# Scores on 64 rows that alternate between the lower and the upper rows of the array

## The chip, the cores and the metric

The kernel runs on one core of a Trainium2 chip. The metric is the time of one execution on the device in microseconds (us). Before the change three runs gave 2135.87, 2143.86 and 2138.03 us, median 2138.03.

The engines are TensorE (PE: matmuls; its weight loads are shown as PEld), VectorE (DVE), ScalarE (ACT), GpSimd (POOL) and SyncE (SP, which issues the loads). They run side by side, each works through its own instructions in order, and a semaphore holds an instruction until what it needs is there.

## The reference

Two transformer blocks of two layers each for 256 tokens of 1024 values, all float32. The change lies in the second block. Each of its layers runs three mixers on one normalised input and joins them:

```python
u = jnp.einsum('btd,de->bte', rmsnorm_2(x, norm1_g[l]), w_in[l])
y_m = mlstm_mixer(...)      # 4 heads of 64: S = (q k^T) * exp(D - m), h = S v / max(|sum S|, exp(-m))
y_a = diff_attention(...)   # 4 heads, each with two halves c of 64:
                            #   p_c = softmax(where(q_pos >= k_pos, q_c k_c^T, -1e30)); o = (p_0 - lam * p_1) v
y_h = hgrn2_mixer(...)      # 4 heads of 64: A[t,s] = sum_k q[t,k] k[s,k] exp(B[t,k] - B[s,k]); o = A v
x = x + concat([y_m, y_a, y_h]) @ w_out[l]
x = x + relu(rmsnorm_2(x, norm2_g[l]) @ w_up[l])**2 @ w_down[l]
```

Each of the scores is a product over 64 values: 64 of the array's 128 rows.

## The kernel before, in words

A weight comes in pieces (`piece`): one DMA into `wraw` (L215), then ScalarE rounds it to `whi` (L226) and VectorE subtracts for the rest, `wlo` (L227). Every large product is three passes of such parts: `gemm_tok` (L247) with tokens on the rows of the result, `gemm_a` (L281) transposed. Their results lie in PSUM banks of the tag "acc"; all small products use the four banks of the tag "sm" (`bank`). A fifth "sm" product must wait until the oldest one's reader is done.

`_second` runs one layer's mixers. A string, `SECOND[l]`, names the order in which the program is written: products (hqf, aq, mvo, ...) and, between them, steps of three generators. `s` is a step of `hgrn_scores`, `a` one of `attention`, `m` one of `mlstm_out`. This is only the written order: the kernel is built with a scheduler (`TileContext(schedule_with_timeline_sim=True)`) that sets the order of the instructions of every engine from its own estimate of times, with the written order as its start. So a change in how a step is written can move its neighbours too.

The operands of two heads, or of the two halves of an attention head, lie above each other: partitions 0 to 63 and 64 to 127. A product over 64 values therefore uses the lower or the upper 64 rows of the array.

- `hgrn_scores`: first `E` and four products per layer (L1540: two on the lower rows into one bank, two on the upper into another), copied by ScalarE (L1541). Then eight levels. A level takes the difference of decay sums (`E`, L1551, L1552), its exponential (ACT, L1553), a product (L1555), and then for the lower rows four matmuls into a bank (L1566) and VectorE's masked copy into `hS` (L1572), and the same again for the upper rows. The last level uses q and k without `E` (`hT`), with 128 columns instead of 64 (copy L1574).
- `mlstm_out`: for each head two matmuls (L1630 256 columns, L1631 128) into one bank and VectorE's product with the weights `wm` (L1632). After two heads come the six products with v (L1638 to L1640).
- `attention`: for each head and each half g: scores of the first 128 queries (L1681), the mask added by a bf16 product of an identity and a matrix of -1e30 (L1682), scores of the other 128 (L1683, 256 columns), the mask (L1684); then VectorE's maximum (L1685, L1686) and bias (L1688) and ScalarE's exponentials (L1690). After both halves the tail of the head before: three transposes of `aa` (L1704), ScalarE's copy `at` (L1706), three products with v (L1708 to L1710), copies (L1712); then the reciprocal of the sums (L1695) and `aa` (L1699). The last head's tail is a step of its own.

After the mixers come `xm`, split from the three outputs (transposes L297), and the product with `w_out`.

Of the kernel before, what the change touches and what calls it, by code (L numbers as in the profile page):

```python
# [10 lines left out]
F32 = mybir.dt.float32  # L11
# [9 lines left out]
D = 1024  # L21
# [3 lines left out]
# ---------------------------------------------------------------- weight pieces  # L25
# A piece is rows [k0, k0 + nk) (in tiles of 128) and columns [c0, c0 + w) of a
# weight, laid out [128, nk, w].
# [45 lines left out]
# ---------------------------------------------------------------- constants of the shapes  # L73
def _consts():
# [19 lines left out]
    for b in (64, 32, 16, 8, 4, 2, 1):  # L94
        j = i[i // b % 2 == 1]   # the queries of this level
        lv.append((i[:, None] // (2 * b) == j[None, :] // (2 * b)) & (i[:, None] // b % 2 == 0))
# [28 lines left out]
# The order of the first block's mixer: products (gt: gates; c, q, v: the delta rule's k, q, v; R, V: retention's q and k,  # L125
# v; g: its output gate; m: merge gates; b: retention's branch; z: the delta rule's output gate), steps of retention (r)
# and of the delta rule (u, k0, L, lv, o, y).
# [4 lines left out]
# The order of the second block's mixer, in its two layers: products (hqf: hgrn2's q, f; hig: its i, g; mvo, mqk: mLSTM's;  # L132
# aq, ak, av: attention's), and steps of hgrn2's scores (s), of attention (a) and of mLSTM (m).
# [4 lines left out]
# Rows of gains, in the order of their use.  # L138
# [4 lines left out]
class Split:  # L143
    """A float32 operand as the sum of two float32r parts."""
# [5 lines left out]
class Kernel:  # L150
# [45 lines left out]
    # ---- weights  # L196
    def piece(self, w, k0, c0, pool=None):
        """Loads a piece of a weight and splits it; with a pool: loads it there, for a later call."""
# [39 lines left out]
    def gemm_tok(self, x, wt, o, tok, k0=0, start=True, stop=True, passes=(0, 1, 2)):  # L238
        """o = x[tok tile] @ w, three passes of float32r parts."""
# [10 lines left out]
    def gemm_b(self, x, w, c0, cb, width=256, n=2, tt=False):  # L250
        """cb(t, x[tok tile t] @ w[:, c0:c0 + n * width]); tt: the first tokens first"""
# [17 lines left out]
    def gemm_a(self, x, wt, ps, first=False):  # L269
        """ps[:, n * 256:+256] = (x @ w[:, n * 128:+128]).T for two n; first: the parts that are ready last come last"""  # L270
# [13 lines left out]
    # ---- activations  # L284
# [5 lines left out]
    def tsplit(self, src, x, t, nk=8, k0=0, scale=None):  # L290
        """x[:, k0:k0+nk, tok tile t] = split(src.T)"""
# [24 lines left out]
    def row(self, name, queue=None):  # L316
        """A vector on all partitions; the next one's load starts."""
# [5 lines left out]
    def rsqrt(self, x, n, scale=1.0, eps=EPS, name="rq"):  # L323
        """(x * scale + eps) ** -0.5 for a narrow x, by Newton's iteration."""
# [17 lines left out]
    def mean_sq(self, x, sq=None):  # L342
        """The mean of x^2 for x [128, D]; sq is overwritten."""
# [25 lines left out]
    def norm_later(self, g, rs, xs=None, sq=(None, None), mid=None):  # L369
        """h * g, transposed (and in xs as it is); rs gets the factors of the tokens that are still to come."""  # L370
# [16 lines left out]
    def along_tokens(self, rs, dg=None):  # L387
        """The factors of the tokens along the columns, on all partitions."""
# [12 lines left out]
    def norm_twice(self, g0, g1, rs):  # L401
        """h = norm(h) * g0; h * g1, transposed, and the factors of its norm."""
# [19 lines left out]
    # ---- first block: mixer  # L422
# [11 lines left out]
    def _mixer(self, l):  # L434
# [5 lines left out]
        if l:   # the factors of the norm come with the products  # L440
# [30 lines left out]
        # ---- the gates of the delta rule, and the first columns of the merge gates  # L471
        gx, beta = one([128, 2, 8], "gx"), one([128, 16], "beta")
        m1 = t8("m1", "xc")   # the merge gates: tanh(x / 2)
# [10 lines left out]
        # ---- the delta rule's k, q, v: convolution, silu, norms  # L484
# [3 lines left out]
        def conv(nm, i):  # L488
# [33 lines left out]
            if nm == "q":  # L522
# [10 lines left out]
                if i == 3:  # L533
                    # of |q|^2, with q's dk ** -0.5
                    G["rq"] = self.rsqrt(qss, 16, scale=128.0, eps=128 * EPS, name="rqq")

        # ---- retention: q, k with rotary, transposed; v; heads
# [58 lines left out]
        # ---- the output gate of retention  # L596
# [13 lines left out]
        # ---- the merge gates, times the branch of retention  # L610
# [22 lines left out]
        # ---- the delta rule's output gate, and its branch  # L633
# [1216 lines left out]
```

## Time and profile before

| | |
|---|---|
| runs, us | 2135.87, 2143.86, 2138.03; median 2138.03 |
| profiled execution, span | 2134.6 us (first to last instruction; no other time of this execution is recorded) |
| instructions | 37091 |
| busy | PE 97%, PEld 90%, DVE 72%, ACT 56%, POOL 2% |
| granted TensorE clock, mean | 0.973 |

The span is read as the time in which the core worked; the runs lie 1.3 to 9.2 us above it. A granted clock of 1.00 is 2.4 GHz and 0.50 is 1.2 GHz. The two mixers of the second block lie at about 1488 to 1560 us (layer 0) and 1840 to 1915 us (layer 1). In a row of the timeline "x2" is the number of hardware instructions: a float32 matmul makes two, a bf16 or float32r matmul one. "64\*128 64x256" is an operand of 64 rows and 128 columns in the array, and 64 rows by 256 columns that stream through it.

### The profile page before, as it was taken

What the parts mean: (1) busy time and instruction counts of PE and PEld (TensorE: products, weight loads), DVE (VectorE), ACT (ScalarE), POOL (GpSimd) and SP (SyncE); (2) the same over time, 40 slices, a digit from 0 to 9 for tenths busy, and PEclk for the clock granted to TensorE, in tenths of its full rate; (3) what the DMA queues carried; (4) which work ended last, traced back from release to release, by engine and by line L of the source; (5) the groups of instructions that cost most, each with busy time, mean ns of one, the idle gap of its engine ahead of it and who ended that gap; (6) DMA issues with size and microseconds to landing.
All of it is one profiled execution on the core that took longest, in us unless ns stands there. A gap on an engine that the chain in (4) does not pass through costs nothing. (4 is left out here: it accounts for less than half of the span.)

```text
span 2134.6 us, 37091 instructions
## 1 busy us (share of the span) xinstructions
PE 2064.5 (97%) x14774; PEld 1928.6 (90%) x14774; DVE 1529.1 (72%) x2848; ACT 1202.5 (56%) x1796; POOL 39.5 (2%) x95
## 2 busy tenths in 40 slices
PE   7999999999999999989999999899899999999999
PEld 7999999999899999988898988789789999888988
DVE  5889576555767996778888888877765448776444
ACT  6554344444564544467787777666535556554554
POOL 0000000000000000000000000020000003000000
PEclk9999899999999999999999999999889999889999
DMA  6454434555544453648999899654225555223553
GB/s 227 161 187 160 127 139 176 195 185 190 188 165 160 175 161 112 218 160 305 332 321 316 322 319 336 233 173 153 80 89 183 193 180 195 101 80 138 181 195 138
DMA packets 82661, 408.14 MB, mean 191 GB/s; under 512 B 25376, under 2 KB 25536, under 8 KB 46768
## 3 DMA queue, kind: packets, MB, share of 16 engines
q1 hardware_dynamic: 61200, 392.19, 51.6%
q0 software_dynamic: 3392, 9.11, 1.4%
q10 hardware_dynamic: 17888, 4.39, 1.0%
q8 instruction: 118, 1.93, 0.4%
q14 instruction: 63, 0.52, 0.1%
HBM read 403.56 MB, written 2.10 MB: 190 GB/s over the span
## 5 line engine op out<-in xcount | busy, mean ns | idle before, releaser
L227 DVE TENSOR_TENSOR wlo<-wraw,whi 128x1024 fp32r<-128x1024 f32 (+3 forms) x644 | 734.4, 1155 | 373.3 <-ACT whi L226 346.5
L226 ACT ACTIVATE whi<-wraw 128x1024 fp32r<-128x1024 f32 (+3 forms) x644 | 633.5, 1005 | 563.7 <-PE acc L247 294.2
L247 PE MATMUL acc<-whi,uhi 128*128 128x256 f32 (+4 forms) x2240 | 609.4, 301 | 9.2 <-ACT uhi L301 4.0
L247 PE MATMUL acc<-wlo,uhi 128*128 128x256 f32 (+4 forms) x2240 | 598.8, 299 | 5.3 <-DVE wlo L227 5.1
L247 PE MATMUL acc<-whi,ulo 128*128 128x256 f32 (+4 forms) x2240 | 602.9, 298 | 0.8 <-DVE ulo L305 0.6
L247 PEld LDWEIGHTS acc<-whi,uhi 128*128 128x128 f32 x2240 | 403.5, 193 | 19.5 <-ACT whi L226 6.6
L247 PEld LDWEIGHTS acc<-wlo,uhi 128*128 128x128 f32 x2240 | 398.2, 191 | 15.2 <-DVE wlo L227 11.4
L247 PEld LDWEIGHTS acc<-whi,ulo 128*128 128x128 f32 x2240 | 400.2, 191 | 5.7 <-DVE ulo L305 1.8
L281 PE MATMUL sm<-uhi,whi 128*128 128x256 f32 x864 | 237.7, 285 | 0.0
L281 PE MATMUL sm<-ulo,whi 128*128 128x256 f32 x864 | 235.9, 282 | 0.0
L281 PE MATMUL sm<-uhi,wlo 128*128 128x256 f32 x864 | 235.1, 281 | 0.0
L227 DVE TENSOR_TENSOR wlo<-xraw,whi 128x704 fp32r<-128x704 f32 (+1 forms) x176 | 165.9, 977 | 38.3 <-ACT whi L226 34.1
L226 ACT ACTIVATE whi<-xraw 128x704 fp32r<-128x704 f32 (+1 forms) x176 | 144.6, 861 | 48.9 <-PE acc L247 14.7
L281 PEld LDWEIGHTS sm<-uhi,whi 128*128 128x128 f32 x864 | 163.8, 195 | 1.6
L281 PEld LDWEIGHTS sm<-ulo,whi 128*128 128x128 f32 x864 | 160.6, 190 | 1.7
L281 PEld LDWEIGHTS sm<-uhi,wlo 128*128 128x128 f32 x864 | 160.4, 189 | 0.0
L247 PE MATMUL acc<-whi,hlo 128*128 128x512 f32 x344 | 135.8, 395 | 0.0
L247 PE MATMUL acc<-wlo,hhi 128*128 128x512 f32 x344 | 135.6, 394 | 0.0
L247 PE MATMUL acc<-whi,hhi 128*128 128x512 f32 x344 | 130.1, 394 | 0.0
L281 PE MATMUL acc<-uhi,whi 128*128 128x256 f32 x448 | 127.3, 284 | 0.0
L281 PE MATMUL acc<-ulo,whi 128*128 128x256 f32 x448 | 126.9, 283 | 0.0
L281 PE MATMUL acc<-uhi,wlo 128*128 128x256 f32 x448 | 126.8, 283 | 0.0
(608 smaller groups left out, 2758.4 us busy)
## 6 DMA issues: line engine op xcount, KB each, us to landing
wraw<-in_w_in SPq DMA_DIRECT2D x80, 1024.0 KB, 4.8
wraw<-in_w_up SPq DMA_DIRECT2D x32, 1024.0 KB, 4.7
wraw<-in_w_down SPq DMA_DIRECT2D x32, 1024.0 KB, 4.7
xraw<-in_exp_w_down SPq DMA_DIRECT2D x24, 1024.0 KB, 7.2
xraw<-in_exp_w_gate SPq DMA_DIRECT2D x32, 704.0 KB, 5.6
xraw<-in_exp_w_up SPq DMA_DIRECT2D x32, 704.0 KB, 5.6
wraw<-in_exp_w_gate SPq DMA_DIRECT2D x32, 704.0 KB, 5.6
wraw<-in_exp_w_up SPq DMA_DIRECT2D x32, 704.0 KB, 5.9
```

Source lines behind the costliest of these rows:

```text
L226: nc.scalar.activation(hi[:, :mm], raw[:, s], AF.Copy)
L227: nc.vector.tensor_tensor(lo[:, :mm], raw[:, s], hi[:, :mm], OP.subtract)
L247: nc.tensor.matmul(o, a[:, k0 + j, ts], b[j], start=start and i == 0 and j == 0, stop=stop and i == 2 and j == n - 1)
L281: self.nc.tensor.matmul(ps[:, n * 256:(n + 1) * 256], a[j][:, n * 128:(n + 1) * 128], b[:, j, :], start=(n, j, i) == one, stop=(n, j, i) = ...
```

## The change

The loops over the row halves go inside: a matmul on the lower rows is followed by the same one on the upper rows. For that both "sm" banks of a pair are taken ahead of the first matmul, and what reads them comes after both. In the attention the four mask products of a head stand together behind its four score products. The rest of the diff removes comments and docstrings, which shifts the line numbers (L1566 is L1567 after it, L1630 and L1631 are L1636, L1632 is L1638, L1681 and L1683 are L1687, L1682 and L1684 are L1690, L1704 is L1712).

```diff
 hgrn_scores
+        ps = [self.bank("sm") for _ in range(2)]
+        for ct in range(2):
+            for pa in range(2):
+                rs = slice(pa * 64, pa * 64 + 64)
+                nc.tensor.matmul(ps[pa][:, ct * 128:(ct + 1) * 128], E3[rs, ct, 0:128], E3[rs, ct, 128:256], start=True, stop=True)
         for pa in range(2):
-            ps = self.bank("sm")
-            rs = slice(pa * 64, pa * 64 + 64)
-            for ct in range(2):
-                nc.tensor.matmul(ps[:, ct * 128:(ct + 1) * 128], E3[rs, ct, 0:128], E3[rs, ct, 128:256], start=True, stop=True)
-            nc.scalar.activation(S2[:, pa], ps[:, 0:256].rearrange("p (c i) -> p c i", c=2), AF.Copy)
+            nc.scalar.activation(S2[:, pa], ps[pa][:, 0:256].rearrange("p (c i) -> p c i", c=2), AF.Copy)
...
+            two = [self.bank("sm") for _ in range(2)]
+            for j in range(4):
+                js = slice(j * 128, (j + 1) * 128)
+                for pa in range(2):
+                    rs = slice(pa * 64, pa * 64 + 64)
+                    nc.tensor.matmul(two[pa][:, j * n:(j + 1) * n], A[rs, js], half(E[rs, js]) if b else fq[rs, js],
+                                     start=True, stop=True)
             for pa in range(2):
-                ps = self.bank("sm")
-                rs = slice(pa * 64, pa * 64 + 64)
-                for j in range(4):
-                    js = slice(j * 128, (j + 1) * 128)
-                    nc.tensor.matmul(ps[:, j * n:(j + 1) * n], A[rs, js], half(E[rs, js]) if b else fq[rs, js], start=True,
-                                     stop=True)
+                ps = two[pa]
                 if b:
 mlstm_out
-            rs_ = slice(pa * 64, pa * 64 + 64)
-            ps = self.bank("sm")
-            nc.tensor.matmul(ps[:, 0:256], mT["k"][rs_, ct, 0:128], mT["q"][rs_, ct, :], start=True, stop=True)
-            nc.tensor.matmul(ps[:, 256:384], mT["k"][rs_, ct, 128:256], mT["q"][rs_, ct, 128:256], start=True, stop=True)
-            nc.vector.scalar_tensor_tensor(wm[:, h, :], ps[:, 0:384], 64.0 ** -0.5, wm[:, h, :], op0=OP.mult, op1=OP.mult)
+            if not pa:
+                two = [self.bank("sm") for _ in range(2)]
+                for o, x, y in ((slice(0, 256), slice(0, 128), slice(0, 256)), (slice(256, 384), slice(128, 256), slice(128, 256))):
+                    for i in range(2):
+                        rs_ = slice(i * 64, i * 64 + 64)
+                        nc.tensor.matmul(two[i][:, o], mT["k"][rs_, ct, x], mT["q"][rs_, ct, y], start=True, stop=True)
+                for i in range(2):
+                    nc.vector.scalar_tensor_tensor(wm[:, h + i, :], two[i][:, 0:384], 64.0 ** -0.5, wm[:, h + i, :], op0=OP.mult, op1=OP.mult)
 attention
+            two = [self.bank("sm") for _ in range(2)]
+            for s, x, y in ((slice(0, 128), slice(0, 128), slice(0, 128)), (slice(128, 384), slice(128, 256), slice(0, 256))):
+                for g in range(2):
+                    gs = slice(g * 64, (g + 1) * 64)
+                    nc.tensor.matmul(two[g][:, s], aT["q"][gs, h, x], aT["k"][gs, h, y], start=s.start == 0, stop=False)
             for g in range(2):
-                gs = slice(g * 64, (g + 1) * 64)
-                ps = self.bank("sm")
-                q, k = aT["q"][gs, h, :], aT["k"][gs, h, :]
-                nc.tensor.matmul(ps[:, 0:128], q[:, 0:128], k[:, 0:128], start=True, stop=False)
-                nc.tensor.matmul(ps[:, 0:128], idb, negb, start=False, stop=True)
-                nc.tensor.matmul(ps[:, 128:384], q[:, 128:256], k, start=True, stop=False)
-                nc.tensor.matmul(ps[:, 256:384], idb, negb, start=False, stop=True)
+                for s in (slice(0, 128), slice(256, 384)):
+                    nc.tensor.matmul(two[g][:, s], idb, negb, start=False, stop=s.start > 0)
+            for g in range(2):
+                ps = two[g]
                 nc.vector.tensor_reduce(mx[:, g, :], ps[:, 0:384].rearrange("p (b i) -> p b i", b=3), axis=AX.X, op=OP.max)
```

The number of instructions of every engine is the same. Up to the second block's first mixer every engine's order is the same too; from there on PE, VectorE and ScalarE differ, POOL and SP do not. Three places show how. In all of them a number behind a name is that of a buffer: two "sm" numbers are two banks, and a bank belongs to one row half.

PE in layer 1, the scores of the first attention head (`aq`, `ak`; `negb`, `idb` are the mask's product), before:

```order
L1681 MATMUL sm_24991<-ak_24438,aq_24641 128x128
L1682 LDWEIGHTS idb_90
L1682 MATMUL sm_24991<-negb_91,idb_90 128x128
L1683 MATMUL sm_24991<-ak_24438,aq_24641 128x256
L1684 LDWEIGHTS idb_90
L1684 MATMUL sm_24991<-negb_91,idb_90 128x128
L1681 MATMUL sm_25001<-ak_24438,aq_24641 128x128
L1682 LDWEIGHTS idb_90
L1682 MATMUL sm_25001<-negb_91,idb_90 128x128
L1683 MATMUL sm_25001<-ak_24438,aq_24641 128x256
L1684 LDWEIGHTS idb_90
L1684 MATMUL sm_25001<-negb_91,idb_90 128x128
```

and after:

```order
L1687 MATMUL sm_24991<-ak_24438,aq_24641 128x128
L1687 MATMUL sm_24992<-ak_24438,aq_24641 128x128
L1687 MATMUL sm_24991<-ak_24438,aq_24641 128x256
L1687 MATMUL sm_24992<-ak_24438,aq_24641 128x256
L1690 LDWEIGHTS idb_90
L1690 MATMUL sm_24991<-negb_91,idb_90 128x128
L1690 LDWEIGHTS idb_90
L1690 MATMUL sm_24991<-negb_91,idb_90 128x128
```

Behind these rows the same two masks follow for the other bank. Heads 0 and 2 of layer 1 stand so; head 1 of layer 1 and head 1 of layer 0 stand with the two products of the lower rows ahead of the two of the upper, and the four masks behind them.

PE in layer 0, levels 0 (its second block) and 1 of `hgrn_scores` (`E`) and the first half of attention head 0, before:

```order
L1566 MATMUL sm_21293<-E_21282 128x64 x4
L1566 MATMUL sm_21304<-E_21299 128x64 x4
L1566 MATMUL sm_21310<-E_21299 128x64 x4
L1681 MATMUL sm_21323<-ak_20959,aq_20565 128x128
L1682 LDWEIGHTS idb_90
L1682 MATMUL sm_21323<-negb_91,idb_90 128x128
L1683 MATMUL sm_21323<-ak_20959,aq_20565 128x256
L1684 LDWEIGHTS idb_90
L1684 MATMUL sm_21323<-negb_91,idb_90 128x128
L281 MATMUL acc_21631<-uhi_20207,whi_21623 128x256
```

and after, from the last two products of the level on:

```order
L1567 MATMUL sm_21304<-E_21299 128x64
L1567 MATMUL sm_21305<-E_21299 128x64
L1687 MATMUL sm_21323<-ak_20959,aq_20565 128x128
L1687 MATMUL sm_21323<-ak_20959,aq_20565 128x256
L1690 LDWEIGHTS idb_90
L1690 MATMUL sm_21323<-negb_91,idb_90 128x128
L1690 LDWEIGHTS idb_90
L1690 MATMUL sm_21323<-negb_91,idb_90 128x128
L281 MATMUL acc_21631<-uhi_20207,whi_21623 128x256
```

The level alternates between its two banks. The scheduler has put the other half of this head (bank sm_21324) twelve large products later, so here one half has both its products and then both its masks. Heads 2 and 3 of layer 0 and head 3 of layer 1 are split in the same way, with other products or the first half's masks between.

VectorE at the end of layer 0's mixer (`amx`, `anb`: maxima and biases of the last attention head; `wm`: mLSTM's scores; `hg`, `E`: hgrn2; `aw`: the reciprocals), before:

```order
L1685 TENSOR_REDUCE amx_21502<-sm_21515 128x3
L1446 TENSOR_SCALAR hx_21859<-acc_21732,r01_20329 128x256
L1686 TENSOR_TENSOR amx_21502<-amx_21502 128x1
L1448 TENSOR_TENSOR hg_20405<-hx_21826,sg_21829 128x256
L1632 SCALAR_TENSOR_TENSOR wm_20930<-sm_21699,wm_20930 128x384
L1686 TENSOR_TENSOR amx_21502<-amx_21502 128x1
L1688 SCALAR_TENSOR_TENSOR anb_21503<-amx_21502,ars_20402 128x2
```

and after:

```order
L1693 TENSOR_REDUCE amx_21502<-sm_21506 128x3
L1552 TENSOR_TENSOR E_21871<-hT_20397 128x256
L1553 TENSOR_TENSOR E_21871<-hT_20397 128x256
L1694 TENSOR_TENSOR amx_21502<-amx_21502 128x1
L1448 TENSOR_TENSOR hg_20405<-hx_21863,sg_21866 128x256
L1694 TENSOR_TENSOR amx_21502<-amx_21502 128x1
L1696 SCALAR_TENSOR_TENSOR anb_21503<-amx_21502,ars_20402 128x2 x2
L1556 TENSOR_TENSOR E_21871<-E_21871,hT_20397 128x512
L1638 SCALAR_TENSOR_TENSOR wm_20930<-sm_21699,wm_20930 128x384
L1638 SCALAR_TENSOR_TENSOR wm_20930<-sm_21700,wm_20930 128x384
L1703 RECIPROCAL aw_21504<-osum_21317 128x4
```

`wm` stood ahead of the maximum and the bias of the second half; it now stands, for both heads, behind them and ahead of the reciprocal.

## Rows read from the trace of the kernel before

**Rows 1.** The page: its span and the busy time of the engines.

```profile
span 2134.6 us, 37091 instructions
...
PE 2064.5 (97%) x14774; PEld 1928.6 (90%) x14774; DVE 1529.1 (72%) x2848; ACT 1202.5 (56%) x1796; POOL 39.5 (2%) x95
```

**Rows 2.** Windows: us, busy PE, PEld, DVE, ACT, POOL, clock, DMA share, GB/s.

```profile
1488.90:1529.50 40.60, 40.60 (x324) 34.96 (x324) 32.73 (x80) 23.84 (x57) 0.00 (x0) 1.00 0.23 81
1529.50:1556.60 27.10, 21.19 (x91) 17.87 (x90) 16.38 (x65) 8.21 (x24) 0.00 (x0) 0.50 0.11 40
1847.10:1898.00 50.90, 50.90 (x395) 45.21 (x393) 39.82 (x109) 29.44 (x70) 0.00 (x0) 0.97 0.29 98
1898.00:1913.00 15.00, 12.64 (x74) 11.68 (x73) 11.89 (x48) 4.60 (x12) 0.00 (x0) 0.62 0.25 91
```

**Rows 3.** Waits of PE in 1529:1557: us in total, times, longest us.

```profile
PE sm L1704 <- DVE aa L1699: 4.7, 1, 4.7
PE sm L1708 <- ACT at L1706: 1.2, 2, 0.6
```

**Rows 4.** Waits of PE in 1898:1913.

```profile
PE sm L1638 <- DVE wm L1632: 2.4, 2, 1.3
```

**Rows 5.** Timeline, PE, layer 0: start us, us, line, operation, operands [idle before].

```profile
1496.33 0.49 PE L1681 MATMUL sm<-ak,aq 64*128 64x128 f32 x2
1496.74 0.23 PE L1682 MATMUL sm<-negb,idb 128*128 128x128 bf16 x1
1496.90 0.70 PE L1683 MATMUL sm<-ak,aq 64*128 64x256 f32 x2
1497.53 0.23 PE L1684 MATMUL sm<-negb,idb 128*128 128x128 bf16 x1
1497.57 0.36 PE L281 MATMUL acc<-uhi,whi 128*128 128x256 f32 x1
...
1498.45 1.60 PE L1566 MATMUL sm<-E 64*128 64x64 f32 x16
1499.98 0.38 PE L281 MATMUL acc<-uhi,whi 128*128 128x256 f32 x1
```

**Rows 6.** Timeline, PE, layer 0: one block of a level by itself.

```profile
1522.91 1.10 PE L1566 MATMUL sm<-E 64*128 64x64 f32 x8
1523.95 0.38 PE L247 MATMUL acc<-whi,uhi 128*128 128x256 f32 x1
```

**Rows 7.** Timeline, PE, layer 1: attention head 0 starts, the level behind it.

```profile
1854.58 0.49 PE L1681 MATMUL sm<-ak,aq 64*128 64x128 f32 x2
...
1857.31 1.60 PE L1566 MATMUL sm<-E 64*128 64x64 f32 x16
```

**Rows 8.** Timeline, PE, layer 1: the scores of two mLSTM heads.

```profile
1898.07 0.71 PE L1630 MATMUL sm<-mq,mk 64*128 64x256 f32 x4
1898.61 0.39 PE L1631 MATMUL sm<-mq,mk 64*128 64x128 f32 x4
```

**Rows 9.** Timeline, PE, the end of layer 0's mixer.

```profile
1529.47 0.76 PE L1704 MATMUL sm<-c_base,aa 128*128 128x128 f32 x3
...
1532.39 1.22 PE L1630 MATMUL sm<-mq,mk 64*128 64x256 f32 x2
...
1538.78 0.99 PE L1704 MATMUL sm<-c_base,aa 128*128 128x128 f32 x3 [4.75 <-DVE aa L1699]
...
1553.61 3.09 PE L1566 MATMUL sm<-hT 64*128 64x128 f32 x16
```

**Rows 10.** Timeline, VectorE, the end of layer 0's mixer.

```profile
1531.26 0.54 DVE L1685 TENSOR_REDUCE amx<-sm 128x3 f32<-128x384 f32 x1
...
1534.07 0.56 DVE L1632 SCALAR_TENSOR_TENSOR wm<-sm,wm 128x384 f32<-128x384 f32 x1 [1.48 <-PE sm L1631]
...
1537.74 0.18 DVE L1695 RECIPROCAL aw<-osum 128x4 f32<-128x4 f32 x1 [0.17 <-ACT pp L1690]
```

**Rows 11.** Timeline, ScalarE, the last head's first exponential.

```profile
1534.81 0.46 ACT L1690 ACTIVATE pp<-sm,anb,ars 128x128 f32<-128x128 f32 x1 [1.02 <-DVE anb L1688]
```

## Prediction

> **What bounds the kernel now.** I read the page's first lines first: TensorE (PE) is busy 2064.5 of 2134.6 us, 97%, VectorE 72%, ScalarE 56% [rows 1]. The change touches only the second block's two mixers, so the stretches in which its lines stand are what counts, and I took the windows there next. In 1488.9–1529.5 (layer 0) and 1847.1–1898.0 (layer 1) PE is busy in all of the time, VectorE in 32.73 of 40.6 and 39.82 of 50.9 us, and the granted clock is 1.00 and 0.97, the 2.4 GHz level [rows 2]: there a microsecond less of PE is a microsecond less of span, as long as nothing else comes late. In 1529.5–1556.6, the end of layer 0's mixer, PE is busy 21.19 of 27.1 us at a granted clock of 0.50, the 1.2 GHz level; in 1898.0–1913.0, the end of layer 1's, 12.64 of 15.0 at 0.62 [rows 2]. The waits of PE in these two name what it waits for: once, 4.7 us, for VectorE's `aa` (the last head's attention weights) [rows 3], and twice, 2.4 us in all, for VectorE's `wm` (mLSTM's weighted scores) [rows 4]. So there are two kinds of term: PE's own time in the full stretches, and a chain over VectorE and ScalarE at the end of layer 0.
>
> **What the array does with 64 rows before the change.** An attention half takes, by the starts of PE's rows, 0.41 us from its first 64-row matmul to the mask, 0.16 to the second 64-row matmul, 0.63 to the second mask and 0.04 to the next full-row product: 1.24 in all [rows 5]. The second 64-row matmul has 128 columns more and takes 0.63 − 0.41 = 0.22 more, so 128 columns cost 0.22 (float32 goes in two passes: x2), and 0.41 − 0.22 = 0.19 is the turn from 64 to 128 rows. Two halves that stand together before the change, with a level behind them, take 1857.31 − 1854.58 = 2.73 [rows 7]. For a level of hgrn2 (8 matmuls, 16 passes), lower block and upper block one after the other take 1499.98 − 1498.45 = 1.53 [rows 5]; one block by itself takes 1523.95 − 1522.91 = 1.04 [rows 6]. Two would be 2.08 in a row, so half of the overlap that the change wants is there already. Two mLSTM heads of 384 columns each, on opposite rows, take 0.93 from the first start to the last end (1898.07 to 1898.61 + 0.39) [rows 8]; by the 0.22 above one of them is 3 × 0.22 = 0.66 of streaming, so they run nearly side by side, although they are written one head after the other.
> The Trainium skill (TensorE: Matmul & The Clock Gate, Part 3: Packing small matmuls — row/col tiling) says that matmuls start and end strictly in program order and that only the loading of weights is pulled ahead. The 0.93 disagrees: upper-row passes start beside lower-row ones that stand ahead of them. By the rule the two attention heads that end up together but not alternating would cost about 0.5 each more, and the sum below would be 1.0 smaller; I go by the trace.
>
> **The change part by part.** No instruction is added or removed; matmuls and weight loads are the same, and the order on PE, VectorE and ScalarE differs only from layer 0's second mixer on.
> 1. *Attention heads whose halves stand together after it* (layer 0 head 1; layer 1 heads 0, 1, 2). Price of a head: 0.93 for two lots of 384 columns [rows 8] and four masks that follow each other, 0.06 each for 128 bf16 columns (bounds: 0.04 by the mask-to-product step, 0.16 by the mask-to-scores step [rows 5]): 1.17. Before: 2 × 1.24 = 2.48 where other products lie between the halves, 2.73 where they are adjacent. Two of each: 2 × 1.31 + 2 × 1.56 = 5.7. With the masks at 0.16: 4.1.
> 2. *Heads that the order still splits* (layer 0 heads 0, 2, 3; layer 1 head 3): 8 halves, in which the two 64-row matmuls now follow each other. Saved is one turn, 0.19, and 0.16 − 0.06 before the second: 0.29 at most, 0.10 at least; I take 0.25, since the 0.19 is the nearer row. 8 × 0.25 = 2.0 (0.8 to 2.3).
> 3. *Levels* (numbered 0 to 7 in their order). Four, level 2 of layer 0 and levels 2, 3, 6 of layer 1, go from block after block to alternating: each from 1.53 to at least 1.04, taken as 1.08, so 4 × 0.45 = 1.8. In layer 0, levels 3 and 4, which overlap each other already, give 0.3, and level 5, whose blocks were apart, 0.5 (bounds 0 and 1.04). Level 0 of layer 0 and levels 1 and 4 of layer 1 stay split by the order, layer 1's level 4 with one block more standing alone; against it stand level 1 of layer 0 and level 5 of layer 1, which now alternate: nothing, with −0.4 to +0.5 around it. The level on hT in layer 0 runs at half clock, 3.09 [rows 9]: eight passes of 128 columns at half clock are 8 × 0.22 = 1.76 of streaming for each row half, side by side and with the offset of two 2.2, so 0.8 with the row's own tail left out. Sum 3.4 (1.8 to 4.5).
> 4. *The end of layer 0.* Before: the transposes of head 2 start on PE at 1529.47, those of the last head at 1538.78, 9.31 later, of which 4.75 idle [rows 9]. In that time VectorE does the last reduce at 1531.26, then reaches `wm`, which waits 1.48 for PE's scores until 1534.07 [rows 10]; behind it in the queue stand the maxima and biases that the exponentials need, so these start only at 1534.81 [rows 11]; 2.93 later, at 1537.74, VectorE takes the reciprocal of their sums, and 1.04 after that PE goes on. After: both `wm` stand behind the biases. The exponentials can start at 1532.1, 0.3 after the reduce's end (1531.26 + 0.54), an estimate: of the two subtractions for E that now stand ahead of the biases nothing is added, since the weight split that stood between the two reduces has moved away. Then the reciprocal is due at 1535.03 and PE at 1536.07. What is late next is `wm` itself: two of 0.56, ahead of the reciprocal and behind both heads' scores, which end at about 1532.39 + 2 × 0.93 (half clock) = 1534.25, so 1535.4 and PE at 1536.4. Of 1538.78 − 1536.4 = 2.4 I take all (bounds: 1.48, the wait alone, and 3.0). The second head's scores, which before followed the last head (one head: 1538.78 − 4.75 − 1532.39 = 1.64 [rows 9]), now lie in PE's idle time: 1.6 more. The other pair joins: 0.2. Sum 4.2.
> 5. *The end of layer 1.* The last head's value products lose the full-row products that lay between them and the transposes, and wait for ScalarE's copy as they do in layer 0, 0.6 each time [rows 3]: −0.6. `wm` comes earlier; of a wait of 2.4 [rows 4] I take 0.95 back. Net +0.35 (−0.6 to +1.8).
> 6. *New waits.* Both banks of a pair are now taken before the first is read, and a bank's reader, the copy to hS or the reduce, comes up to one block later. Behind a PE that waits there stand all the products of its queue. The cover is the lead that VectorE has at 81% and 78% of the two stretches [rows 2]; gone once in each mixer, this costs about one block's half: −1.0 (0 to −4).
> Sum: 5.7 + 2.0 + 3.4 + 4.2 + 0.35 − 1.0 = 14.65, taken as 14.5. The profiled execution spans 2134.6; its own time beyond that isn't recorded. The median of the runs, 2138.03, lies 3.4 above it, and I keep that: 2134.6 − 14.5 + 3.4 = 2123.5. All bounds low: 4.1 + 0.8 + 1.8 + 1.5 + 1.6 − 0.6 − 4 = 5.2; all high: 5.7 + 2.3 + 4.5 + 4.8 + 1.8 = 19.1.
>
> **The rivals.**
> *A. PE only comes sooner to what others have not done.* VectorE at 81% and the weight halves it splits for every product lie in the same stretches [rows 2]; where they have no lead, PE's shorter scores turn into waits, and of parts 1 to 3 (11.1) little is left. Against it: PE waits for nothing in either full stretch. Left are parts 4 and 5 and some of the rest, about 5: 2133.
> *B. It doesn't do what it says.* The order splits four of eight heads and some levels, and the array already lets opposite rows overlap [rows 8]. If joined heads go no faster either, parts 1 and 3 vanish and the waits of 6 remain: −2, 2136. Against it: the turns of 0.19 are real rows [rows 5].
> *C. Slower: the clock falls sooner.* The granted clock is 1.00 up to 1529.5 with PE busy throughout and 0.50 behind it, where PE waits [rows 2]. Row halves side by side, and waits between them, leave PE less occupied in the same stretch. Work of x us at full clock that then lies at half takes x more: it decides from x = 14.5 on, that is if the fall comes at 1515 rather than 1529.5. With both mixers' last 13 us at half: 2123.5 + 26 = 2150. Against it: the products between the scores are untouched, and 0.97 stood through layer 1's scores.
> *D. More.* All bounds at their good end, and with the shorter idle time the clock comes back sooner within the 27.1 us at 0.50: −21, 2117.
>
> **How the numbers follow.** Forecast 0.56, A 0.24, B 0.06, C 0.05, D 0.09. A run of this kernel tells 0.5%, 10.7 us, from no change: faster means under 2127.3, slower over 2148.7. The forecast's own range is 2118 to 2129, with 0.04 of its chance above 2127.3; so faster is 0.52 + 0.09 + 0.03 (of A) = 0.64, slower 0.05 (C), same 0.31. The range reaches from D to A: 2113 to 2135.
>
> **What would show it.** Right: the attention scores of layer 1's heads 0 to 2 and layer 0's head 1 take about 1.2 us from the first 64-row matmul to the next full-row product; a level takes about 1.1; PE's wait for `aa` in layer 0 falls from 4.7 to about 2, with the exponentials' start no longer behind `wm`; and PE's busy time falls by about 11. Wrong: new PE waits for hS, `amx` or weight halves in the full stretches (A); joined heads at 2.4 (B); a granted clock of 0.50 before the last head's scores (C).

## The result, and the profile after

The changed kernel took 2113.06 us (median of five runs, 2111.22 to 2118.89) against 2138.03: ratio 0.989, 95% interval 0.9871 to 0.9909. So it is faster, as forecast, by 25 us where 14.5 were forecast. Over 60 runs of the kernel before, taken beside the experiments below, and 11 of the changed one, the mean spans are 2138.2 and 2112.5 us, and the mean granted clocks 0.9740 and 0.9809.

The page's first lines after (busy us, share of the span, instructions), beside [rows 1]:

```profile
span 2117.1 us, 37095 instructions
...
PE 2048.4 (97%) x14774; PEld 1916.2 (91%) x14774; DVE 1528.7 (72%) x2848; ACT 1203.8 (57%) x1796; POOL 39.9 (2%) x95
```

PE is busy 16.1 us less, where the prediction said about 11; the other engines do what they did. This profiled execution is the slowest of the five runs.

The windows after, with the columns of [rows 2]: layer 0's mixer up to head 2's transposes, its end, and layer 1's mixer up to the last head's transposes, and its end (the third window starts with the mixer, the one in [rows 2] 7.3 us into it):

```profile
1485.50:1521.07 35.57, 35.50 (x323) 31.57 (x322) 33.35 (x82) 25.14 (x61) 0.00 (x0) 1.00 0.30 106
1521.07:1543.72 22.65, 19.34 (x98) 17.04 (x99) 15.52 (x64) 7.47 (x22) 0.00 (x0) 0.58 0.12 44
1826.10:1878.30 52.20, 52.20 (x467) 48.80 (x467) 46.00 (x128) 35.09 (x78) 0.00 (x0) 1.00 0.32 111
1878.30:1893.60 15.30, 11.24 (x91) 10.26 (x90) 13.77 (x53) 7.06 (x17) 0.00 (x0) 0.88 0.28 105
```

From the first S2 product to the first product of hgrn2's output, layer 0's mixer takes 58.2 us (1485.51 to 1543.72) instead of 69.5 (1488.89 to 1558.40), layer 1's 67.5 instead of 74.9: 18.7 us less in the mixers, where the spans differ by 17.5. In layer 1 the two stretches do not hold the same work: 184 full-row products of L247 stand in it after, 166 before, because the first S2 product now stands ahead of 18 of them. At 0.12 us each that is 2.1 us, so for the same work the mixers are about 20.8 us shorter. The full stretches are still full, with VectorE now at 94% and 88%, and PE waits for no semaphore in them. At the end of layer 0 the clock is 0.58 instead of 0.50, at the end of layer 1 0.88 instead of 0.62 [rows 2].

Part of that last gain has only moved. The first 10 us behind layer 1's mixer, before and then after:

```profile
1914.71:1924.71 10.00, 10.00 (x56) 8.69 (x56) 7.54 (x35) 3.90 (x6) 0.00 (x0) 0.97 0.01 2
```

```profile
1893.63:1903.63 10.00, 10.00 (x37) 8.94 (x37) 5.58 (x31) 1.89 (x4) 0.00 (x0) 0.50 0.01 2
```

The clock now falls later (at 1890 us, 11.7 after the last head's transposes start, where before it fell 6 after them) and stays low behind the mixer. From there to the end of the program the changed kernel takes 223.5 us instead of 219.9.

PE's timeline after in layer 1, attention head 0 and the level behind it (start us, us, line, operation, operands), beside [rows 7]:

```profile
1841.40 0.93 PE L1687 MATMUL sm<-ak,aq 64*128 64x128 f32 x8
1842.25 0.40 PE L1690 MATMUL sm<-negb,idb 128*128 128x128 bf16 x4
1842.58 1.11 PE L1567 MATMUL sm<-E 64*128 64x64 f32 x16
1843.62 0.39 PE L281 MATMUL acc<-uhi,whi 128*128 128x256 f32 x1
```

The head takes 1842.58 − 1841.40 = 1.18 instead of 2.73, the level 1.04 instead of 1.53 [rows 5]. In layer 0, the second half of head 0, split from the first, and level 2:

```profile
1492.42 0.92 PE L1687 MATMUL sm<-ak,aq 64*128 64x128 f32 x4
1493.27 0.28 PE L1690 MATMUL sm<-negb,idb 128*128 128x128 bf16 x2
1493.36 0.36 PE L281 MATMUL acc<-uhi,whi 128*128 128x256 f32 x1
...
1494.36 1.11 PE L1567 MATMUL sm<-E 64*128 64x64 f32 x16
1495.40 0.38 PE L281 MATMUL acc<-ulo,whi 128*128 128x256 f32 x1
```

A half takes 0.94 instead of 1.24 [rows 5]. PE's waits at the end of layer 0 and then of layer 1 (us in total, times, longest), beside [rows 3, 4]:

```profile
PE sm L1712 <- DVE aa L1707: 1.6, 1, 1.6
PE sm L1716 <- DVE amx L1693: 0.7, 1, 0.7
PE sm L1716 <- ACT at L1714: 0.6, 1, 0.6
PE sm L1636 <- ACT mix L1720: 0.4, 1, 0.4
```

```profile
PE sm L1644 <- DVE wm L1638: 2.2, 2, 1.5
PE sm L1716 <- ACT at L1714: 1.8, 1, 1.8
```

And PE's timeline at the end of layer 0, beside [rows 9]:

```profile
1521.07 0.55 PE L1712 MATMUL sm<-c_base,aa 128*128 128x128 f32 x3
...
1522.32 0.49 PE L1716 MATMUL sm<-av,at 128*128 128x128 f32 x2 [0.70 <-DVE amx L1693]
1522.64 0.39 PE L1717 MATMUL sm<-av,at 128*128 128x128 f32 x2
...
1523.18 0.92 PE L1636 MATMUL sm<-mq,mk 64*128 64x256 f32 x4
1524.49 1.36 PE L1636 MATMUL sm<-mq,mk 64*128 64x256 f32 x4 [0.39 <-ACT mix L1720]
1527.48 0.99 PE L1712 MATMUL sm<-c_base,aa 128*128 128x128 f32 x3 [1.64 <-DVE aa L1707]
...
1539.94 2.09 PE L1567 MATMUL sm<-hT 64*128 64x128 f32 x16
```

The last head's transposes start 6.41 after head 2's instead of 9.31, and the level on hT takes 2.09 instead of 3.09, at half clock in both kernels. The first products behind head 2's transposes still run at full clock (0.32 from L1716 to L1717), where before the same two products stood 0.59 apart, at half clock. The last head's first exponential, and VectorE's second `wm` and the reciprocal, beside [rows 10, 11]:

```profile
1524.33 0.46 ACT L1698 ACTIVATE pp<-sm,anb,ars 128x128 f32<-128x128 f32 x1
```

```profile
1525.88 0.56 DVE L1638 SCALAR_TENSOR_TENSOR wm<-sm,wm 128x384 f32<-128x384 f32 x1 [0.47 <-PE sm L1636]
1526.45 0.18 DVE L1703 RECIPROCAL aw<-osum 128x4 f32<-128x4 f32 x1
```

The exponentials now start ahead of both `wm`.

### The profile page after: what moved, and what is told of

The parts are those of the page before. It is cut to its first block, busy times and chain, and to the rows that moved or that the text cites. A ratio compares the mean times of both kernels' runs of the same rounds, so it can differ in the third digit from the quotient of the medians.

```text
span 2117.1 us, 37095 instructions
## 1 busy us (share of the span) xinstructions
PE 2048.4 (97%) x14774; PEld 1916.2 (91%) x14774; DVE 1528.7 (72%) x2848; ACT 1203.8 (57%) x1796; POOL 39.9 (2%) x95
## 3 DMA queue, kind: packets, MB, share of 16 engines
q8 instruction: 118, 1.93, 0.4%
## 5 line engine op out<-in xcount | busy, mean ns | idle before, releaser
L247 PE MATMUL acc<-whi,uhi 128*128 128x256 f32 (+4 forms) x2240 | 609.4, 301 | 8.8 <-ACT uhi L301 4.1
L247 PE MATMUL acc<-whi,ulo 128*128 128x256 f32 (+4 forms) x2240 | 603.3, 298 | 0.8 <-DVE ulo L305 0.6
L247 PE MATMUL acc<-wlo,uhi 128*128 128x256 f32 (+4 forms) x2240 | 598.2, 299 | 3.7 <-DVE wlo L227 3.0
L247 PEld LDWEIGHTS acc<-whi,uhi 128*128 128x128 f32 x2240 | 402.6, 192 | 19.5 <-ACT whi L226 6.3
L247 PEld LDWEIGHTS acc<-wlo,uhi 128*128 128x128 f32 x2240 | 397.7, 191 | 14.3 <-DVE wlo L227 10.4
L247 PEld LDWEIGHTS acc<-whi,ulo 128*128 128x128 f32 x2240 | 400.1, 191 | 6.0 <-DVE ulo L305 1.8
L247 PE MATMUL acc<-whi,hlo 128*128 128x512 f32 x344 | 135.8, 395 | 0.0
L247 PE MATMUL acc<-wlo,hhi 128*128 128x512 f32 x344 | 135.6, 394 | 0.0
L247 PE MATMUL acc<-whi,hhi 128*128 128x512 f32 x344 | 130.1, 394 | 0.0
```

What stands on the lines that cost most here:

```text
L247: nc.tensor.matmul(o, a[:, k0 + j, ts], b[j], start=start and i == 0 and j == 0, stop=stop and i == 2 and j == n - 1)
```

## The experiments

All of them change the second block's two mixers only, in the kernel before or in the changed one. "Mixer" is the stretch from the first S2 product to the first product of hgrn2's output.

**The changed kernel again**, beside more runs of the kernel before.

> The changed kernel once more, beside the kernel before. Theory P (PE's own time): the mixers' two stretches are 11.3 and 7.4 us shorter in every execution, the rest is the same, so runs differ by 18 to 19 us, and where a pair of runs differs by more, the rest of the program differs too. Theory K (clock): the 25 us between the first medians hold some 6 us that come from the granted clock; then executions of either kernel differ among themselves by 2 us for each 0.001 of mean clock, the changed kernel lies at 0.978 to 0.982 and the one before at 0.973 to 0.976, and the difference of medians is again over 20 us.

Measured: 2115.38 against 2139.03, ratio 0.9886 (0.9855 to 0.9916). The mixers take 57.5 and 67.3 us, 18.9 to 19.6 less than the two traces of the kernel before show (the second of them is the last run below). Over all kernels of the study with several runs, spans of one kernel fall by 1.85 us for each 0.001 of its mean clock (0.9 to 2.6 by kernel). By that, of −25.7 us between the mean spans, 0.0069 × 1850, about 13, would go with the clock and 13 would not. This is a rough estimate: clock and waits hang together, a shorter stretch at half clock raises the mean clock by itself, and the slope comes from executions of one kernel and is carried here from one kernel to another. Theory K's difference of over 20 us came, and its 2 us for each 0.001 holds for the kernel before (1.93), not for the changed one (0.93 in 11 runs); the clocks scatter more than it said, 0.969 to 0.979 and 0.978 to 0.984. Theory P's 18 to 19 us lie at the edge of the interval (18 to 31). The two traces of each kernel place about 18 us: some 21 in the mixers for the same work, less 3 behind the second one, which takes 223.3 us to the end here too. The 7 to 8 us that are left of the 25.7 they do not place.

**The parts alone.** Each of the three functions as changed, the other two as before (`attention`, `hgrn_scores`, `mlstm_out`).

> Only the attention's part of the change; levels and mLSTM as before. By its order two heads stand joined (layer 1, heads 0 and 2) and twelve halves are split, and VectorE's wm moves behind the biases at the end of layer 0. Theory P: 12 x 0.30 + 2 x 1.55 + 2.9 = 9.6 us less (2126 to 2130 where before is 2138). Theory K: the clock adds 2 to 4 us to it, with a mean granted clock 0.001 to 0.002 above that of the kernel before. Rival (nothing from the attention itself, all from the other two): under 3 us.

> Only hgrn2's levels and the S2 scores alternate; attention and mLSTM as before. wm moves behind the biases here too. Theory P: levels 0.48 + 0.33 + 1.0 + 1.0 (hT) in layer 0, about 1.5 in layer 1, 2.9 at the end of layer 0: 7.2 us less. Without the moved wm: 4.3. Theory K: 2 to 4 us on top, by the clock.

> Only mLSTM's heads are scored in pairs; attention and levels as before. By its order wm still stands ahead of one of the two maxima, so the wait for aa should stay near 4.7 less the 1.6 that the second head's scores now take in it. Theory P: 1.6 to 2 us less. Rival (the pairs carry the tail's gain): 4.5 us less or more.

Measured against 2139.03: 2124.83 (ratio 0.9935, 0.9905 to 0.9965), 2130.2 (0.9958, 0.9939 to 0.9976) and 2133.27 (0.9977, 0.9956 to 0.9998). The three differences are 14, 9 and 6, with intervals of about ±6, ±4 and ±4; that their sum, 29, is more than the 25 of all of them is within the noise. But one piece is seen in two of them, in PE's waits at the end of layer 0, attention alone, levels alone, mLSTM alone:

```profile
PE sm L1706 <- DVE aa L1701: 2.9, 1, 2.9
```

```profile
PE sm L1707 <- DVE aa L1702: 2.7, 1, 2.7
```

```profile
PE sm L1707 <- DVE aa L1702: 4.1, 1, 4.1
```

With either of the first two the scheduler puts `wm` behind the biases, as with the whole change, and the wait of 4.7 [rows 3] loses 1.8 to 2.0; with mLSTM alone it doesn't, and the wait falls to 4.1 where 3.1 was expected. The attention is the largest part. The mean clocks were 0.9767, 0.9773 and 0.9758, over the 0.9740 of the kernel before. Each part gains more than theory P's sum (14.2 for 9.6, 8.8 for 7.2, 5.8 for 1.6 to 2), but each sum lies within the interval, so theory K's surplus isn't shown here. For mLSTM alone the time is nearer the rival's 4.5, and its place is open: in its trace the two mixers take 67.0 and 81.3 us, together 4 more than before (15 more full-row products stand in the second, whose clock is 0.85 where it was 0.89).

**Alternation, or only standing together.** In `attention`:

```diff
-            for s, x, y in (...):
-                for g in range(2):
+            for g in range(2):
+                for s, x, y in (...):
                     nc.tensor.matmul(two[g][:, s], aT["q"][gs, h, x], aT["k"][gs, h, y], ...)
```

> The changed kernel, but a head's attention scores are written lower, lower, upper, upper, masks together as before; on PE only layer 1's heads 0 and 2 differ from the changed kernel, whose four products take 0.86 us from the first to the first mask. Theory O (opposite rows overlap out of the written order): 0.86 again. Theory F (matmuls start and end in the order written): 128 columns and 256 columns, twice, one after the other, 4 x 0.22 + 2 x 0.22 = 1.32, so 1.3 to 1.5.

PE's timeline, layer 1, head 0:

```profile
1842.39 0.93 PE L1687 MATMUL sm<-ak,aq 64*128 64x128 f32 x8
1843.26 0.40 PE L1690 MATMUL sm<-negb,idb 128*128 128x128 bf16 x4
```

0.87 to the first mask: theory O. Layer 0's head 1, which the changed kernel itself has in this order, takes 0.86 there too. With four passes of the lower rows ahead, the upper rows' passes run beside them all the same; for the attention the alternation itself is worth nothing. For the longer blocks of a level it is worth something: eight passes of the lower rows and then eight of the upper, with nothing between them, took 1.53 before the change [rows 5], alternating they take 1.04. The rule of the Trainium skill that the prediction weighed (TensorE: Matmul & The Clock Gate, Part 3), that matmuls start and end in program order, would by the rows' prices have given about 1.3 here, an estimate; the row decides. (One run, 2116.8.)

**The masks apart again**: each pair of score products followed by its masks, still alternating and in two banks.

> The changed kernel, but each pair of score products is followed by its masks, so a head turns between 64 and 128 rows three times instead of once, and a split half as often as in the kernel before. Theory T (the turns are what the attention's part saves): a split half takes 1.24 again instead of 0.94, a joined head about 0.86 + 0.2 + 0.16 + masks 0.23 = 1.45 instead of 1.1; 12 x 0.3 and more, some 4 us of the mixers' stretches. Rival S (side by side is what it saves, turns are free): joined heads stay at 1.1 to 1.2, split halves as well at 0.94.

PE's timeline, layer 0's split half and layer 1's head 2:

```profile
1494.27 0.48 PE L1688 MATMUL sm<-ak,aq 64*128 64x128 f32 x2
1494.68 0.23 PE L1690 MATMUL sm<-negb,idb 128*128 128x128 bf16 x1
...
1495.51 0.37 PE L281 MATMUL acc<-uhi,whi 128*128 128x256 f32 x1
...
1857.09 0.49 PE L1688 MATMUL sm<-ak,aq 64*128 64x128 f32 x4
1857.51 0.29 PE L1690 MATMUL sm<-negb,idb 128*128 128x128 bf16 x2
...
1858.48 0.39 PE L1712 MATMUL sm<-c_base,aa 128*128 128x128 f32 x2
```

The half is back at 1.24, the head at 1.39 instead of 1.10 to 1.18; the mixers take 60.2 and 71.7, 2 and 4 us more. The second is no clean measure of the turns: that mixer holds 18 full-row products fewer than the changed kernel's, and its clock was 0.90, where the changed kernel's were 0.97 and 0.98. Theory T: what the attention saves is, first, that the two halves of a head stand together (2.73 to about 1.4), and then the turns (1.39 to 1.1; 1.24 to 0.94).

**One order undone.** VectorE's `wm` of the first head is made to stand ahead of the second half's maximum in layer 0, with an edge of order only. (Layer 0's PE order stays, but the scheduler moved PE's order in layer 1 along with it: 18 full-row products left that mixer, and one head there is split again.)

```diff
+                    if h + i == 0 and mng_l == 0:
+                        self.tc.add_manual_dep(self.late.ins, ins.ins.name, ...)   # late: the last head's second maximum
```

> The changed kernel with one order undone: at the end of layer 0 VectorE is made to do the first head's wm ahead of the second half's maximum, as in the kernel before; PE's order there is that of the changed kernel. Theory Q (the chain from VectorE's queue sets the last head's transposes): only the second half's exponentials are late, by wm's wait for PE and its 0.56, so the wait for aa goes from 1.6 to 2.1 up to 3 to 4.5 us and layer 0's mixer from 57.5 to 58.2 up to 59.5 to 61. Rival: the exponentials had slack, the wait stays at about 2 and the mixer under 58.5; then the tail's gain came from PE's order and the clock alone.

PE's wait and VectorE's rows behind the biases of the first half:

```profile
PE sm L1714 <- DVE aa L1709: 2.9, 1, 2.9
```

```profile
1531.58 0.56 DVE L1638 SCALAR_TENSOR_TENSOR wm<-sm,wm 128x384 f32<-128x384 f32 x1 [0.63 <-PE sm L1636]
...
1533.97 0.18 DVE L1705 RECIPROCAL aw<-osum 128x4 f32<-128x4 f32 x1 [1.16 <-ACT pp L1700]
```

The reciprocal now waits 1.16 for the exponentials, layer 0's mixer takes 59.7, 1.5 to 2.3 us more: theory Q, at its small end (the wait, 2.9, lies just under the 3 to 4.5 it said, and well over the rival's 2). Seven runs have a median of 2122.15 (ratio 0.9921, 0.9892 to 0.9949, which touches the changed kernel's 0.9871 to 0.9909), some 7 us over the changed kernel, with a mean clock of 0.9763. In this trace the clock at the end of layer 0 is 0.52, down already at the first products behind head 2's transposes. So the order costs about 2 us in layer 0's mixer. The rest of the 7 can be the clock's or layer 1's moved order; this run doesn't separate them.

**Full-row work in the tails.** First, full-row products of the program held back into them, 24 and 48 of hgrn2's 96 for i and g (the step moved in the order, with an edge from the mLSTM scores to the first product of the held group):

> The changed kernel, but the last 24 of the 96 full-row products of hgrn2's i and g are held back on PE until the first mLSTM pair's scores, in both layers, so that they lie in the waits for aa and wm at the end of the mixer. Theory K (the granted clock follows how full the tail is with full-row products): the tails' half-clock time falls from 14 to 27 us in layer 0 and 10 to 14 in layer 1 to under half of it, and the kernel is 6 to 10 us faster than the changed kernel (2105). Theory P: the clock stays, only 1.6 to 3 us of waits in each layer are filled: 3 to 4 us faster. Rival: hg and hv come later than hgrn2's output wants them: no gain or slower.

> As held1, with 48 products held back (5.6 us at full clock), more than the waits can hold. Theory K: the clock stays up in more of the tail, 6 to 12 us faster than the changed kernel. Theory P: 3 us of them only push aa's transposes back, so no better than held1, rather 2 us worse.

Measured 2123.58 and 2132.74, ratios 0.9923 (0.9897 to 0.9949) and 0.9946 (0.9928 to 0.9965): both behind the changed kernel's 0.989, as the rival says (with 24 the intervals still touch). With 24 the clock at the end of layer 0 was 0.78, and the wait for aa gone there. Layer 0's mixer took 57.6, as in the changed kernel, and layer 1's 74.1, 6.7 more: new waits turned up, at the end of layer 0 and of layer 1:

```profile
PE sm L1575 <- DVE E L1564: 2.4, 1, 2.4
PE sm L1724 <- ACT at L1722: 2.0, 2, 1.4
```

```profile
PE sm L1575 <- DVE E L1564: 4.8, 1, 4.8
```

The steps' moved order lets `E` come late. Then products that nobody reads, which take nothing from elsewhere: in columns 384 to 512 of banks that are held anyway,

```diff
+    def fill(self, ps, a, b, n):
+        for i in range(n):
+            self.nc.tensor.matmul(ps[:, 384:512], a, b, start=True, stop=True)
```

> The changed kernel with extra products whose results nobody reads: float32, all 128 rows, 128 columns, 0.22 us each at full clock, 9 behind the first mLSTM pair's scores, 6 behind the second's, 5 behind the last head's transposes, in each layer: 4.4 us of PE a layer, most of it where PE waits. Theory K (waits and half-used rows in the tail lower the clock): the half-clock time in the tails (layer 0: 27 and 14 us, layer 1: 14 and 10 in the two traces) falls to half or less, 3 to 8 us faster than the changed kernel. Theory W (the clock does not heed them): they cost what sticks out of the waits, 1 to 4 us slower.

> The changed kernel with fewer unread products and in layer 0 only: 6 behind each mLSTM pair's scores, 4 behind the last head's transposes, 0.22 us each at full clock. From the run with 20 in each layer: layer 0's mixer 55.5 to 57 us (57.5 to 58.2 without), layer 1's as in the changed kernel, 67.4. The kernel 1 to 3 us faster than the changed one, which is within what can be measured; if the clock falls in layer 0's tail all the same, no gain.

Windows of layer 0's end, from head 2's transposes to hgrn2's output: the kernel before (its second trace), the changed kernel (its second trace), with 20 such products, with 16 in layer 0 alone:

```profile
1530.27:1559.08 28.81, 22.91 (x99) 19.56 (x100) 17.16 (x66) 8.83 (x25) 0.00 (x0) 0.50 0.11 37
```

```profile
1522.00:1544.63 22.63, 18.83 (x103) 16.30 (x102) 16.07 (x66) 7.65 (x23) 0.00 (x0) 0.70 0.14 47
```

```profile
1524.86:1545.91 21.05, 19.55 (x139) 17.41 (x139) 14.38 (x63) 7.31 (x22) 0.00 (x0) 0.84 0.13 49
```

```profile
1520.65:1539.97 19.32, 16.42 (x131) 14.02 (x131) 14.22 (x63) 7.31 (x22) 0.00 (x0) 1.00 0.15 53
```

The clock is 0.50, 0.70 (0.58 in the first trace, and 0.54 in the run with the scores unalternated, whose layer 0 is the same), 0.84, 1.00, the last two in one trace each, and the stretch shrinks from 22.6 to 21.1 and 19.3, though it holds 28 to 36 more of PE's instructions. Over all runs the mean clocks are 0.986 and 0.984, over the 0.981 of the changed kernel. So the unread products go with a higher clock, as theory K says. The times don't follow: 2112.28 (ratio 0.9867, 0.9840 to 0.9894) and 2114.61 (0.9882, 0.9850 to 0.9914), which can't be told from the changed kernel's 0.989, where theory K had 3 to 8 us. The products' own time takes part of it, and in the second run the clock was lost again elsewhere: its layer 0 mixer took 54.9 us, under the 55.5 to 57 expected, but layer 1's, where nothing was added, took 70.3 where 67.4 was expected. There the clock fell in the middle of the full stretch, with PE busy throughout, behind a level and attention scores that take 64 rows:

```profile
1858.00:1866.00 8.00, 8.00 (x41) 7.22 (x40) 6.29 (x18) 3.32 (x9) 0.00 (x0) 0.57 0.01 2
```

A higher clock at one place is so not a faster kernel by itself.

**The kernel before, once more.**

> The kernel before, for a second trace of it. If the clock's share of the gain lies in the two mixers, their stretches take 69.5 and 74.9 us again, within 2 us, with 30 us at half clock at the end of layer 0; if it is chance in the rest of the program, the mixers differ by as much as the rest, 3 to 5 us.

Its mixers took 69.4 and 74.4 us (69.5 and 74.9 in the first trace), with the clock at 0.50 in layer 0's end again. The mixers' 19 us are the change's. The stretch behind the second mixer takes 220.5 us, near the 219.9 of the first trace, so the 3 us that are given back there after the change are seen in both pairs. The stretch between the mixers differs among executions (281.4 and 284.9 before, 282.4 and 276.2 after, the 18 moved products included).

## Why the prediction was right, and what it mis-sized

The time lies in the range, 0.06 us above its lower end, and outside the forecast's own 2118 to 2129; that it is inside at all is luck, since the five runs reach from 2111.22 to 2118.89. The mechanism is the one forecast. Rival A falls: the full stretches got no wait. Rival B falls: joined heads went from 2.73 to 1.18. Rival C falls for this kernel: the clock is 1.00 in both full stretches, in both traces of it; what it feared is seen in the trace with 16 unread products. Rival D had one of its two grounds half right: the clock is better at the ends, but in layer 0's it fell later rather than came back sooner.

By the steps of the sum:

- *Joined heads* (1.17 forecast): 1.10 to 1.18. Right; layer 0's head 1 1.41 less, layer 1's heads 0 and 2 1.55 less each.
- *Split halves* (0.25 forecast): 0.30, so 2.4 instead of 2.0.
- *Levels* (1.08 forecast): 1.04 to 1.05; levels 3 and 4 0.34 less, hT 1.0 less. Right, but for level 6 of layer 1. The prediction priced it before the change at 1.53, the price at full clock, though it lies in the stretch with a clock of 0.62 and took 2.39 there; it takes 1.04 after:

```profile
1901.09 2.47 PE L1566 MATMUL sm<-E 64*128 64x64 f32 x16
1903.48 0.69 PE L1638 MATMUL sm<-mv,wm 128*128 128x66 f32 x2
...
1883.95 1.11 PE L1567 MATMUL sm<-E 64*128 64x64 f32 x16
1884.99 0.44 PE L1644 MATMUL sm<-mv,wm 128*128 128x66 f32 x2
```

- *The end of layer 0* (4.2, and 0.8 for hT): 28.93 to 22.65, 6.3 instead of 5.0. The chain was right: wait for aa 1.6 where "about 2" was said, PE on at 6.41 where the working gives 1536.4 − 1529.47 = 6.9. `wm` was late next, as said: VectorE takes the reciprocal right behind its second one, at 1526.45. Of the surplus, 0.5 lies ahead of the last head's transposes, where the first 3.8 us ran at full clock. The other 0.8 lies behind them, at half clock before and after: hT gives 0.2 more than forecast, level 6 of this layer, which the sum left out, 0.2, and the value products 0.5, of which more now stand next to each other.
- *The end of layer 1* (0.35, with 0.45 for level 6): 18.81 to 15.32 from the last head's transposes on, of which 1.1 are nine full-row products that now stand ahead: 2.4 instead of 0.8. Here the step failed. The wait for `at` came (1.8, more than the 0.6 assumed) and that for `wm` stayed (2.2 of 2.4), so PE waits 4.1 us where it waited 2.4. The gain is the half clock's, 0.88 for 0.62, and the 10 us behind the mixer pay for it.
- *New waits* (−1.0): none.

Beside these the clock of layer 1's full stretch, 0.97 before and 1.00 after in both pairs of traces, is in no step. Together it is 18.7 in the mixers, 20.8 for the same work, for 14.65 forecast; 3 are given back behind the second mixer. The rest of the 25, 7 to 8 us, the forecast hadn't, and two traces of each kernel don't place it. The mis-sized term is the clock: the sum took it as the profile before had it, but for level 6, and gave it no term of its own. What makes it better after the change isn't shown. The unread products show that more full-row work at layer 0's end goes with a higher clock there; but layer 1's end is less full after the change (PE busy 11.24 of 15.30 us, before 12.64 of 15.0 [rows 2]) and its clock is higher all the same. That the clock makes some 13 of the 25 us is an estimate from runs at different clocks; the unread products, with a clock 0.003 to 0.005 higher and no clear gain, speak for less.

## What to carry to other kernels

Where half-height matmuls share the array, look first for what stands between them: full-row work, even a mask of 0.05 us, costs a turn each way and keeps two row halves from running side by side (a head 2.73 us before, 1.18 after). The order within the pair counted for nothing in blocks of four passes, and for a third of the time in blocks of eight (1.53 to 1.04). Where a change shortens a stretch at half clock, price it twice, at the old clock and at the full one, put the second into the range, and measure the stretch behind it too: half clock can move there. And where a scheduler orders the queues, compare the order of the waiting engines: here about 2 us came from an instruction on VectorE that moved even where its own lines were not edited (the attention's and the levels' part alone).

## What the runs showed of the hardware

- Passes on the upper rows start beside passes on the lower rows that stand ahead of them in the order: eight passes written lower, lower, upper, upper take 0.87, alternating 0.86. In blocks of eight passes for each half that is so only in part: 1.53 in a row, 1.04 alternating, 1.04 for one block alone [rows 5, 6].
- A turn from 64 to 128 rows costs 0.41 − 0.22 = 0.19, the way back 0.16 less the mask's own 0.05. It costs the same for two passes as for four on both halves (0.41 and 0.42 from the first score to the mask, with the masks apart).
- The granted clock of one and the same stretch differs between executions of one kernel (0.58 and 0.70 at the end of layer 0). With unread full-row products in it, it was 0.84 and 1.00.
- The clock can fall to half where PE waits for nothing: 0.57 in 1858 to 1866 us of the run with 16 unread products, PE busy in all of the 8 us.
